# First operands loaded in halves and a shorter warm-up, in a hybrid-mixer layer

## The chip, the cores and the metric

The kernel runs on one core of a Trainium2 chip. The core has a matrix engine (TensorE, PE in the profile, with its weight loads as PEld), three engines for elementwise work (VectorE, DVE; ScalarE, ACT; GpSimd, POOL), a queue engine (SyncE, SP) that mostly starts transfers, and 16 DMA engines. The metric is the device time of one execution in microseconds.

## The reference

One layer, input x of 512 tokens by 1024 channels in float32. What matters here is its front:

```python
h = rmsnorm(x, norm_g[l])                      # x * rsqrt(mean(x*x) + eps) * g
p = jnp.einsum('btd,dc->btc', h, w_in[l])      # one input projection for all branches
(gq, gk, gv, gz, ggate, dq, dk, dv, dgate, qi, ki, wi, pu, pgate) = split_cols(p)
...                                            # gated linear attention, top-k attention, pooling
y = jnp.concatenate([y_gla, y_dsa, y_pool], axis=-1)
x = x + jnp.einsum('btc,cd->btd', y, w_out[l])
```

The output is a final rmsnorm of x. Every product is wanted at about float32 accuracy, so the kernel splits each operand into a high and a low part and multiplies three times: high by high, high weights by low tokens, low weights by high tokens.

## The kernel before

The projection is worked in column chunks. The first chunk of 512 columns (`FIRST`: the linear attention's q and k, the index k and some small pieces) is done in `open_run`, while the input is still arriving; the other chunks follow in `project`. In `open_run` the 1024 channels are 8 blocks, k = 0 to 7, of 128 channels. A block is a piece of x transposed, `xk` (128 channels by 512 tokens; `x0` for k = 0, with the eight columns of norm_g behind it), and a piece of the weights, `wk` (128 channels by 512 columns), 256 KB each. `load_x` and `load_w` start the transfers, wk0 and wk1 from ScalarE's queue, the others from SP's.

For each block `split` makes four operands: the high weights `whk` (ScalarE, `hi_of`, L96), the high tokens `hTh` (VectorE for k = 0, L958; ScalarE after that, L956), the low tokens `hTl` (VectorE, L959) and the low weights `wlk` (VectorE, `lo_of`, L99). In the text a number behind a name is the block: wlk2 is `wlk` of block 2. `square` lets ScalarE square x (L965) and GpSimd add the squares to `acc` (L967). `products` issues twelve matmuls per block, three parts by four groups of 128 tokens, into four accumulators `pns` (`pf` in the profile), each 128 tokens by 512 columns, filled over all eight blocks. Ahead of the first product come four products of ones in plain float32 (`warm`, L994), which nothing reads. After block 7, `rms` sums `acc` over the channels (`ss`, L980) and takes the power −0.5 on GpSimd (`rstd`, L983); `store_first` scales the four accumulators out to `ki` and `kq` (L272, L274), which are then transposed (L306, L299), and the index products `is` (L436) use the result.

The order on each engine is fixed when the program is built: TensorE's stream of block products is interleaved there with products of the next chunk, `qd` (`pt_qd`, L208 to L210), by a timeline that the builder works out. SP issues its transfers in the order of the code. Transfers on the hardware queues share eight semaphores in turn, DMAHW0 to DMAHW7, so a transfer waits for the one issued eight places before it.

Of the kernel before, what the change touches and what calls it, by code (L numbers as in the profile page):

```python
# [69 lines left out]
def hybrid_layer(  # L70
# [16 lines left out]
    def S(tag, shape, dt=F32, bufs=1, name=None):  # L87
        return sb.tile(shape, dt, tag=tag, name=name or tag, bufs=bufs)
# [6 lines left out]
    def hi_of(dst, src, scale=1.0):  # L95
        nc.scalar.activation(dst, src, AF.Copy, scale=scale)  # L96
# [832 lines left out]
    def open_run():  # L929

        xs, ws, wh, wl = {}, {}, {}, {}
        acc = S("acc", [P, T])
        pns = [PS("ov", [P, T], 1, name="pf0"), PS("sc", [P, T], 2, name="pf1"), PS("sc", [P, T], 2, name="pf2"),
               PS("pj", [P, T], 3, name="pf3")]
        ht = lambda parts, k: parts[k // 4][:, k % 4, :]
        x0 = S("x0", [P, T + KT])
        g_of = lambda k: x0[:, T + k:T + k + 1]

        def load_x(k):
            if k == 0:  # L940
                xs[0] = x0[:, 0:T]
                nc.sync.dma_start(x0, block(x_t, 0, T + KT))
                return
            xs[k] = S("xk", [P, T], bufs=5, name=f"xk{k}")
            nc.sync.dma_start(xs[k], block(x_t, k * P * T + P * KT, T))

        def load_w(k, eng=nc.sync):
            ws[k] = S("wk", [P, T], bufs=5, name=f"wk{k}")
            eng.dma_start(ws[k], block(w_in, k * P * T, T))

        def split(k):
            wh[k] = S("whk", [P, T], F32R, bufs=3, name=f"whk{k}")
            wl[k] = S("wlk", [P, T], F32R, bufs=3, name=f"wlk{k}")
            hi_of(wh[k], ws[k])
            if k:
                nc.scalar.activation(ht(hTh, k), xs[k], AF.Copy, scale=g_of(k))  # L956
            else:
                nc.vector.tensor_scalar(ht(hTh, k), xs[k], g_of(k), None, op0=ALU.mult)  # L958
            nc.vector.scalar_tensor_tensor(ht(hTl, k), xs[k], g_of(k), ht(hTh, k).bitcast(F32),  # L959
                                           op0=ALU.mult, op1=ALU.subtract)  # L960
            lo_of(wl[k], ws[k], wh[k])

        def square(k):
            q = acc if k == 0 else S("sqk", [P, T], bufs=2, name=f"sqk{k}")
            nc.scalar.activation(q, xs[k], AF.Square)  # L965
            if k:
                nc.gpsimd.tensor_tensor(acc, acc, q, op=ALU.add)  # L967

        def products(k, parts=range(3)):
            for part in parts:  # L970
                a, w = ht(hTl if part == 1 else hTh, k), (wl if part == 2 else wh)[k]
                for t in range(NT):
                    mm(pns[t], a[:, t * P:(t + 1) * P], w, start=(k + part == 0),  # L973
                                    stop=(k == KT - 1 and part == 2))

        def rms():

            ss = PS("tp", [P, NT], 2, name="ss")
            for t in range(NT):
                mm(ss[:, t:t + 1], acc[:, t * P:(t + 1) * P], ones[:, 0:1], start=True, stop=True,  # L980
                   skip_group_check=True)
            nc.vector.tensor_scalar(rstd, ss, 1.0 / D, EPS, op0=ALU.mult, op1=ALU.add)
            nc.gpsimd.tensor_tensor(rstd, rstd, half_neg, op=ALU.pow)  # L983

        load_x(0)
        load_w(0, nc.scalar)
        for k in range(1, KT):
            load_w(k, nc.scalar if k == 1 else nc.sync)
            load_x(k)
        nc.sync.dma_start(tab, table)  # L990
        load_next()
        load_next()
        for n in (4, 4, 2, 1):
            mm(warm[:, 0:n * P], ones, ones4[:, 0:n, :], start=True, stop=True)  # L994
        split(0)
        square(0)
        for k in range(KT - 1):
            products(k)
            if k + 1 < KT:
                split(k + 1)  # L1000
                square(k + 1)
            if k == 4:
                split_half(chunks[0], 0)
            if k == 6:
                split_half(chunks[0], 1)
                products(7, (0,))
                rms()
                half("n1", 0)
                products(7, (1, 2))
        for t in range(NT):  # L1010
            store_first(t, pns[t])
        rms_diag()
        store_rest()
# [59 lines left out]
def _x_blocks(x_t, norm_g):  # L1073

    import numpy as np

    first = np.concatenate([x_t[0:P], norm_g.reshape(KT, P).T], axis=1)
    return np.concatenate([first.reshape(-1), x_t[P:].reshape(-1)])


def _blocks(w, cols):
# [6 lines left out]
def _layout(i):  # L1088
# [4 lines left out]
    return {  # L1093
        "in_x": i["x"],
        "in_x_t": _x_blocks(i["x"][0].T, i["norm_g"][0]),
        "in_w_in": np.concatenate([w_in[:, FIRST].reshape(-1)] + [_blocks(w_in, cols) for _, cols in CHUNKS]),
        "in_w_out": np.concatenate([_blocks(w_out, list(range(256 * j, 256 * j + 256))) for j in range(4)]),
        "in_rel_bias": _bias_layout(i["rel_bias"]),
        "in_table": _small_layout(i["gla_gate_w2"], i["gla_gate_b"], i["gla_norm_g"], i["pool_w"], i["pool_scale"]),
# [26 lines left out]
```

## Time and profile before

| | |
|---|---|
| three runs | 262.27 us median, 262.04 to 262.34 |
| profiled execution | 262.02 us, span 260.2 us |
| TensorE busy | 245.0 us (94% of the span) |
| VectorE, ScalarE, GpSimd busy | 197.4, 119.6, 103.3 us |
| chain that ended last | TensorE 47%, VectorE 36%, waits without a cause shown 6%, ScalarE 4%, DMA 3% |

A busy time says how long an engine was at work, not whether the end waited for it. That is in the chain that ended last, which is followed back from the last instruction through whatever released each step. Matmul ends are modelled and overlap, so the distance from one start to the next tells the pace.

### The profile page before, as it was taken

The page shows a single profiled execution, that of the slowest core. Times are in us where ns is not written, and L with a number is a line of the kernel's source. Part 1 is how long each engine was busy: PE and PEld are TensorE (multiplying, and loading weights), DVE is VectorE, ACT ScalarE, POOL GpSimd, SP SyncE. Part 2 cuts the span into 40 slices and gives each one's busy share as a digit, 9 for nine tenths or more (in the row PEclk, how much of TensorE's full clock was granted, in tenths as well). Part 3 has the DMA queues.
Part 4 walks back from the last instruction along what each step waited for, and adds up shares of the span by engine and source line. Part 5 has one row for each costly group of instructions (what it writes and reads, how often), then busy time and mean ns, then how long its engine had stood idle before and what let it go on. Part 6 is the DMA issues. An engine that isn't in the chain of part 4 may idle for free.

```text
span 260.2 us, 4199 instructions
## 1 busy us (share of the span) xinstructions
PE 245.0 (94%) x1498; PEld 203.8 (78%) x1498; DVE 197.4 (76%) x442; ACT 119.6 (46%) x251; POOL 103.3 (40%) x109
## 2 busy tenths in 40 slices
PE   8999999999999999899999989998989978999990
PEld 4778889999999998688888867776756755788890
DVE  3999388899999999998999853599875877345322
ACT  5965186884836722225323353434465745222111
POOL 1645356354058630418534063618456562000011
PEclk9999999999999999999999999999999999999997
DMA  6994413225202150222314867605486000025012
GB/s 229 393 410 174 128 46 97 79 78 214 81 1 89 74 165 0 81 82 81 90 74 115 195 136 174 273 0 131 141 217 239 4 0 0 3 98 215 35 58 81
DMA packets 11780, 31.09 MB, mean 119 GB/s; under 512 B 1600, under 2 KB 1600, under 8 KB 11760
## 3 DMA queue, kind: packets, MB, share of 16 engines
q1 hardware_dynamic: 11328, 30.05, 36.2%
q10 hardware_dynamic: 432, 0.79, 0.9%
q8 instruction: 12, 0.20, 0.3%
q14 instruction: 8, 0.07, 0.1%
HBM read 23.91 MB, written 2.10 MB: 100 GB/s over the span
## 4 chain that ended last, share of the span: by engine, by line
PE 47%; DVE 36%; issue 6%; ACT 4%; DMA 3%; POOL 2%; SPq 1%; POOLq 0%; ACTq 0%; DVEq 0%
PE op L772 11%; DVE scs L459 8%; DVE m L458 6%; PE pf L973 5%; DVE ol L99 3%; PE pt_c L210 2%; PE pt_c L208 2%; PE pt_c L209 2%; DVE pm L583 2%; PE ov L741 2%; DMA wk<-in_w_in 2%; PE tpp L730 2%; ACT L L712 2%; DVE wl_n L99 2%; DVE wlk L99 2%
## 5 line engine op out<-in xcount | busy, mean ns | idle before, releaser
L721 POOL TENSOR_SCALAR L<-L,ast 128x128 f32<-128x128 f32 (+3 forms) x24 | 14.8, 630 | 34.1 <-DVE ast L719 34.1
L458 DVE MAX8 m<-scs 128x8 f32<-128x256 f32 (+2 forms) x48 | 26.5, 552 | 0.1
L459 DVE MATCH_REPLACE8 scs<-m,scs 128x256 f32<-128x256 f32 (+2 forms) x48 | 26.1, 543 | 0.0
L196 PE MATMUL pn_n<-wh_n,hTh 128*128 128x270 f32 (+1 forms) x128 | 21.6, 291 | 0.0
L196 PE MATMUL pn_n<-wl_n,hTh 128*128 128x270 f32 (+1 forms) x128 | 21.1, 287 | 0.0
L196 PE MATMUL pn_n<-wh_n,hTl 128*128 128x270 f32 (+1 forms) x128 | 21.0, 286 | 0.0
L712 ACT ACTIVATE L<-L,ast 128x128 f32<-128x128 f32 (+3 forms) x24 | 13.3, 557 | 16.0 <-DVE ast L710 15.1
L208 PE MATMUL pt_c<-hTh,wh_c 128*128 128x512 f32 x48 | 19.3, 402 | 0.0
L210 PE MATMUL pt_c<-hTh,wl_c 128*128 128x512 f32 x48 | 19.0, 395 | 0.0
L209 PE MATMUL pt_c<-hTl,wh_c 128*128 128x512 f32 x48 | 18.9, 394 | 0.0
L196 PEld LDWEIGHTS pn_n<-wh_n,hTh 128*128 128x128 f32 x128 | 18.2, 189 | 0.7 <-issue 0.4
L196 PEld LDWEIGHTS pn_n<-wl_n,hTh 128*128 128x128 f32 x128 | 18.0, 189 | 0.0
L196 PEld LDWEIGHTS pn_n<-wh_n,hTl 128*128 128x128 f32 x128 | 18.0, 189 | 0.0
L99 POOL TENSOR_TENSOR wl_c<-wr_c,wh_c 128x1024 fp32r<-128x1024 f32 x5 | 11.9, 2399 | 12.5 <-ACT wh_c L96 8.2
L967 POOL TENSOR_TENSOR acc<-acc,sqk 128x512 f32<-128x512 f32 x7 | 10.3, 1475 | 11.2 <-ACT sqk L965 11.2
L96 ACT ACTIVATE yDh<-yt 128x128 fp32r<-128x128 f32 x12 | 3.7, 310 | 21.8 <-DVE yt L744 21.8
L744 DVE TENSOR_TENSOR yt<-ov,dg 128x128 f32<-128x128 f32 x12 | 3.4, 285 | 13.2 <-PE ov L741 13.2
L99 POOL TENSOR_TENSOR wl_n<-wr_n,wh_n 128x1080 fp32r<-128x1080 f32 (+1 forms) x4 | 10.1, 2536 | 7.1 <-ACT wh_n L96 5.1
L689 POOL TENSOR_TENSOR L<-scs,TB 128x512 f32<-128x512 f32 x9 | 12.9, 1436 | 0.0
L778 ACT ACTIVATE sqo<-xr 128x512 f32<-128x512 f32 (+1 forms) x8 | 4.8, 604 | 16.9 <-DVE xr L777 10.6
L558 POOL TENSOR_TENSOR gss<-gss,hneg 128x4 f32<-128x4 f32 x4 | 4.1, 1014 | 21.4 <-DVE gss L557 21.4
L99 DVE TENSOR_TENSOR ol<-wr_wo,oh 128x512 fp32r<-128x512 f32 x16 | 11.2, 744 | 1.3 <-ACT oh L96 1.3
(241 smaller groups left out, 711.1 us busy)
## 6 DMA issues: line engine op xcount, KB each, us to landing
wr_wo<-in_w_out SPq DMA_DIRECT2D x8, 512.0 KB, 4.5
wr_c<-in_w_in SPq DMA_DIRECT2D x6, 512.0 KB, 3.9
wr_n<-in_w_in SPq DMA_DIRECT2D x4, 540.0 KB, 7.8
wr_n<-in_w_in SPq DMA_DIRECT2D x4, 536.0 KB, 3.5
xr<-in_x SPq DMA_DIRECT2D x4, 512.0 KB, 6.3
xk<-in_x_t SPq DMA_DIRECT2D x7, 256.0 KB, 5.5
wk<-in_w_in SPq DMA_DIRECT2D x6, 256.0 KB, 5.4
KK<-qkh SPq DMA_DIRECT2D x12, 128.0 KB, 2.5
```

The costliest lines, as they stand in the source:

```text
L99: return (eng or nc.vector).tensor_tensor(dst, src, hi.bitcast(F32), op=ALU.subtract)
L196: mm(ps[:, 0:n], a[:, k, ts_], w[:, k, :], start=(h + part + k == 0), stop=(h == 1 and part == 2 and k == 3))
L208: mm(ps[:, t0:T], c.hi[h][:, k, cs], hTh[h][:, k, t0:T], start=(h + k == 0), stop=False)
L209: mm(ps[:, t0:T], c.hi[h][:, k, cs], hTl[h][:, k, t0:T], start=False, stop=False)
L210: mm(ps[:, t0:T], c.lo[h][:, k, cs], hTh[h][:, k, t0:T], start=False, stop=(h == 1 and k == 3))
L458: nc.vector.max(out=m8, in_=msk[i])
L459: nc.vector.match_replace(out=msk[i], in_to_replace=m8, in_values=msk[i], imm_value=TAKEN)
L689: nc.gpsimd.tensor_tensor(L[:, :, near], msk[i][:, near].unsqueeze(1).to_broadcast([P, 2, 256]), TB[:, 2 * g:2 * g + 2, :], op=ALU.subtract)
L712: nc.scalar.activation(L[:, b, 0:n], L[:, b, 0:n], AF.Exp, bias=st[:, b:b + 1], scale=-1.0, accum_out=st[:, 2 + b:3 + b])
L721: nc.gpsimd.tensor_scalar(L[:, b, 0:n], L[:, b, 0:n], st[:, 4 + b:5 + b], 1.0, op0=ALU.mult, op1=ALU.mult)
L772: mm(outs[t][a][:, 0:e - a], lhs, rhs, start=(first and yi == 0 and rhs is wh and lhs is yh), stop=(last and yi == len(ys) - 1 and lhs is yl))
L973: mm(pns[t], a[:, t * P:(t + 1) * P], w, start=(k + part == 0), stop=(k == KT - 1 and part == 2))
```

## The change

Block 0 of x and of the weights comes in two transfers each, and the host lays the bytes out so that each half is contiguous (the gains g now stand in front of the first half of x0). Block 0's high weights and high tokens are made in two halves of 256 columns. The four products of high by high of block 0 become eight of 256 columns, the first tokens and the first weight columns first. Of the four warm-up products, the two of 256 and 128 columns are dropped.

```diff
-        x0 = S("x0", [P, T + KT])
-        g_of = lambda k: x0[:, T + k:T + k + 1]
+        x0 = S("x0", [P, KT + T])
+        g_of = lambda k: x0[:, k:k + 1]
+        H = T // 2
 
         def load_x(k):
             if k == 0:
-                xs[0] = x0[:, 0:T]
-                nc.sync.dma_start(x0, block(x_t, 0, T + KT))
+                xs[0] = x0[:, KT:KT + T]
+                nc.sync.dma_start(x0[:, 0:KT + H], block(x_t, 0, KT + H))
+                nc.sync.dma_start(x0[:, KT + H:KT + T], block(x_t, P * (KT + H), H))
                 return
...
         def load_w(k, eng=nc.sync):
             ws[k] = S("wk", [P, T], bufs=5, name=f"wk{k}")
+            if k == 0:
+                for a in (0, H):
+                    eng.dma_start(ws[0][:, a:a + H], block(w_in, a * P, H))
+                return
             eng.dma_start(ws[k], block(w_in, k * P * T, T))
 
         def split(k):
...
-            hi_of(wh[k], ws[k])
             if k:
+                hi_of(wh[k], ws[k])
                 nc.scalar.activation(ht(hTh, k), xs[k], AF.Copy, scale=g_of(k))
             else:
-                nc.vector.tensor_scalar(ht(hTh, k), xs[k], g_of(k), None, op0=ALU.mult)
+                for a in (0, H):
+                    hi_of(wh[0][:, a:a + H], ws[0][:, a:a + H])
+                    nc.vector.tensor_scalar(ht(hTh, 0)[:, a:a + H], xs[0][:, a:a + H], g_of(0), None, op0=ALU.mult)
...
         def products(k, parts=range(3)):
             for part in parts:
                 a, w = ht(hTl if part == 1 else hTh, k), (wl if part == 2 else wh)[k]
+                if k + part == 0:
+                    for t, c in ((0, 0), (1, 0), (0, H), (1, H), (2, 0), (3, 0), (2, H), (3, H)):
+                        mm(pns[t][:, c:c + H], a[:, t * P:(t + 1) * P], w[:, c:c + H], start=(c == 0), stop=False,
+                           skip_group_check=True)
+                    continue
                 for t in range(NT):
-                    mm(pns[t], a[:, t * P:(t + 1) * P], w, start=(k + part == 0),
-                                    stop=(k == KT - 1 and part == 2))
+                    mm(pns[t], a[:, t * P:(t + 1) * P], w, start=False, stop=(k == KT - 1 and part == 2),
+                       skip_group_check=True)
...
-        for n in (4, 4, 2, 1):
+        for n in (4, 4):
             mm(warm[:, 0:n * P], ones, ones4[:, 0:n, :], start=True, stop=True)
```

TensorE's stream at its start, before (`warm` is the warm-up, `pf0` to `pf3` the accumulators, `whk0` and `hTh0` the high parts of block 0):

```order
L994 MATMUL warm_68<-ones_63 128x512 x2
L994 MATMUL warm_68<-ones_63 128x256
L994 MATMUL warm_68<-ones_63 128x128
L973 MATMUL pf0_143<-whk0_192,hTh0_77 128x512
L973 MATMUL pf1_144<-whk0_192,hTh0_77 128x512
L973 MATMUL pf2_145<-whk0_192,hTh0_77 128x512
L973 MATMUL pf3_146<-whk0_192,hTh0_77 128x512
```

And with the change:

```order
L1007 MATMUL warm_68<-ones_63 128x512 x2
L982 MATMUL pf0_143<-whk0_192,hTh0_77 128x256
L982 MATMUL pf1_144<-whk0_192,hTh0_77 128x256
L982 MATMUL pf0_143<-whk0_192,hTh0_77 128x256
L982 MATMUL pf1_144<-whk0_192,hTh0_77 128x256
L982 MATMUL pf2_145<-whk0_192,hTh0_77 128x256
```

Two warm-up products are gone, and the first four products need the first half of the tokens only, the first two of them the first half of the weight columns only.

SP's queue at its start, before, with what each transfer waits for (`x` is block 0 of x):

```order
L942 DMA x_147<-in_x_t 128x520
L945 DMA xk_153<-in_x_t 128x512
L949 DMA wk_155<-in_w_in 128x512
L945 DMA xk_157<-in_x_t 128x512
L949 DMA wk_159<-in_w_in 128x512
L945 DMA xk_161<-in_x_t 128x512
L949 DMA wk_163<-in_w_in 128x512 [waits DMAHW0_49]
```

And with the change:

```order
L943 DMA x_147<-in_x_t 128x264
L944 DMA x_147<-in_x_t 128x256
L947 DMA xk_155<-in_x_t 128x512
L955 DMA wk_157<-in_w_in 128x512
L947 DMA xk_159<-in_x_t 128x512
L955 DMA wk_161<-in_w_in 128x512 [waits DMAHW0_49]
L947 DMA xk_163<-in_x_t 128x512 [waits DMAHW1_49]
```

Two transfers of block 3 (wk_161 and xk_163 here) now wait, for the first half of wk0 and of x0; from wk4 on each waits for the same landing as before.

TensorE's stream around the sum of squares `ss`, before (`pt_qd` is the next chunk, `whk_320` block 6, `whk_341` block 7):

```order
L973 MATMUL pf_146<-whk_320,hTh_78 128x512
L210 MATMUL pt_qd_407<-hTh_77,wl_qd_305 128x384 [waits DVE_49]
L208 MATMUL pt_qd_407<-hTh_77,wh_qd_304 128x384
L209 MATMUL pt_qd_407<-hTl_79,wh_qd_304 128x384
L210 MATMUL pt_qd_407<-hTh_77,wl_qd_305 128x384
L208 MATMUL pt_qd_407<-hTh_77,wh_qd_304 128x384
L973 MATMUL pf_143<-whk_320,hTl_80 128x512 [waits DVE_49]
...
L973 MATMUL pf_146<-whk_341,hTh_78 128x512
L209 MATMUL pt_qd_407<-hTl_79,wh_qd_304 128x384
L980 MATMUL ss<-ones,acc 128x1 [waits Pool_49]
```

And with the change (from the fifth `pt_qd` product of the piece on, `whk_326` is block 6 and `whk_347` block 7):

```order
L208 MATMUL pt_qd_413<-hTh_77,wh_qd_310 128x384
L209 MATMUL pt_qd_413<-hTl_79,wh_qd_310 128x384
L210 MATMUL pt_qd_413<-hTh_77,wl_qd_311 128x384
L208 MATMUL pt_qd_413<-hTh_77,wh_qd_310 128x384
L209 MATMUL pt_qd_413<-hTl_79,wh_qd_310 128x384
L986 MATMUL pf_143<-whk_326,hTl_80 128x512 [waits DVE_49]
...
L986 MATMUL pf_146<-whk_347,hTh_78 128x512
L210 MATMUL pt_qd_413<-hTh_77,wl_qd_311 128x384
L208 MATMUL pt_qd_413<-hTh_78,wh_qd_356 128x384 [waits Activation_49]
L209 MATMUL pt_qd_413<-hTl_80,wh_qd_356 128x384
L993 MATMUL ss<-ones,acc 128x1 [waits Pool_49]
```

Of the `pt_qd` products, nine instead of five stand between block 6's first and second part, and three instead of one directly ahead of `ss`: six more in front of it, and six fewer behind. Elsewhere the order on every engine is the same.

## Rows read from the trace of the kernel before

**Rows 1.** Chain that ended last, 0 to 37 us: start, us, what.

```profile
1.21 4.53 DMA wk<-in_w_in
...
5.76 0.64 ACT whk L96
...
14.54 1.78 DVE wlk L99
...
16.37 6.80 PE pf L973 x28
```

**Rows 2.** Timeline, TensorE, 0 to 22 us: start, us, engine, line, operation [idle before].

```profile
5.20 1.17 PE L973 MATMUL pf<-whk,hTh 128*128 128x512 f32 x4
...
11.81 1.09 PE L973 MATMUL pf<-whk,hTl 128*128 128x512 f32 x4
12.98 1.20 PE L973 MATMUL pf<-wlk,hTh 128*128 128x512 f32 x4
...
14.92 1.07 PE L973 MATMUL pf<-whk,hTl 128*128 128x512 f32 x4
16.37 1.21 PE L973 MATMUL pf<-wlk,hTh 128*128 128x512 f32 x4 [0.38 <-DVE wlk L99]
```

**Rows 3.** Timeline, VectorE, 0 to 22 us.

```profile
4.25 0.49 DVE L958 TENSOR_SCALAR hTh<-x 128x512 fp32r<-128x512 f32 x1 [3.25 <-DMA x<-in_x_t]
...
7.04 0.75 DVE L959 SCALAR_TENSOR_TENSOR hTl<-xk,x,hTh 128x512 fp32r<-128x512 f32 x1 [0.92 <-ACT hTh L956]
7.71 1.80 DVE L99 TENSOR_TENSOR wlk<-wk,whk 128x512 fp32r<-128x512 f32 x1
...
11.14 1.79 DVE L99 TENSOR_TENSOR wlk<-wk,whk 128x512 fp32r<-128x512 f32 x1
```

**Rows 4.** Timeline, ScalarE, 0 to 22 us.

```profile
4.42 0.63 ACT L96 ACTIVATE whk<-wk 128x512 fp32r<-128x512 f32 x1 [1.77 <-DMA wk<-in_w_in]
4.96 0.62 ACT L965 ACTIVATE acc<-x 128x512 f32<-128x512 f32 x1
5.76 0.64 ACT L96 ACTIVATE whk<-wk 128x512 fp32r<-128x512 f32 x1 [0.19 <-DMA wk<-in_w_in]
```

**Rows 5.** Timeline, GpSimd, 0 to 22 us.

```profile
7.62 1.35 POOL L967 TENSOR_TENSOR acc<-acc,sqk 128x512 f32<-128x512 f32 x1 [6.32 <-ACT sqk L965]
```

**Rows 6.** Timeline, TensorE's weight loads, 0.9 to 5.6 us.

```profile
3.76 0.34 PEld L994 LDWEIGHTS warm<-ones 128*128 128x128 f32 x1 [0.52 <-issue]
4.61 0.64 PEld L994 LDWEIGHTS warm<-ones 128*128 128x128 f32 x3 [0.52 <-issue]
```

**Rows 7.** DMA, 8 to 13 us, then 17 to 20 us: packets moved.

```profile
DMA packets 1087, 1.98 MB, mean 397 GB/s; under 512 B 118, under 2 KB 118, under 8 KB 1087
...
DMA packets 329, 1.25 MB, mean 416 GB/s; under 512 B 40, under 2 KB 40, under 8 KB 329
```

**Rows 8.** Windows: length, busy by engine, granted clock, DMA share, GB/s.

```profile
1.50:2.75 1.25, 1.25 (x2) 0.37 (x2) 0.00 (x0) 1.14 (x2) 0.00 (x0) 1.00 0.74 169
2.75:5.25 2.50, 2.50 (x8) 1.26 (x6) 0.97 (x2) 0.83 (x2) 0.00 (x0) 1.00 1.02 375
```

**Rows 9.** Chain and timelines around the sum of squares: TensorE, GpSimd and VectorE.

```profile
31.07 0.18 PE pt_qd L210
...
28.16 0.95 PE L980 MATMUL ss<-ones,acc 128*128 128x1 f32 x8
...
29.38 2.02 POOL L983 TENSOR_TENSOR rstd<-rstd,hneg 128x4 f32<-128x4 f32 x1 [6.52 <-DVE rstd L982]
...
32.55 0.74 DVE L274 TENSOR_SCALAR kq<-pf,rstd 128x512 f32<-128x512 f32 x1
...
34.16 1.04 PE L299 MATMUL tpn<-ident,kq 128*128 128x128 f32 x8
...
38.85 0.40 PE L436 MATMUL is<-KS,QS 96*128 96x256 f32 x2
```

**Rows 10.** Window 35 to 60 us.

```profile
35.00:60.00 25.00, 25.00 (x164) 22.67 (x163) 22.30 (x43) 19.87 (x37) 11.29 (x15) 1.00 0.22 70
```

More of the change, by code (lines that the diff above doesn't have):

```diff
@@ L1075, in _x_blocks, with _first @@
     import numpy as np
-    first = np.concatenate([x_t[0:P], norm_g.reshape(KT, P).T], axis=1)
-    return np.concatenate([first.reshape(-1), x_t[P:].reshape(-1)])
+    first = np.concatenate([norm_g.reshape(KT, P).T, x_t[0:P, 0:T // 2]], axis=1)
+    return np.concatenate([first.reshape(-1), x_t[0:P, T // 2:].reshape(-1), x_t[P:].reshape(-1)])
+def _first(w):
+    import numpy as np
+    return np.concatenate([w[0:P, 0:T // 2].reshape(-1), w[0:P, T // 2:].reshape(-1), w[P:].reshape(-1)])
 def _blocks(w, cols):
@@ L1095, in _layout @@
         "in_x_t": _x_blocks(i["x"][0].T, i["norm_g"][0]),
-        "in_w_in": np.concatenate([w_in[:, FIRST].reshape(-1)] + [_blocks(w_in, cols) for _, cols in CHUNKS]),
+        "in_w_in": np.concatenate([_first(w_in[:, FIRST])] + [_blocks(w_in, cols) for _, cols in CHUNKS]),
         "in_w_out": np.concatenate([_blocks(w_out, list(range(256 * j, 256 * j + 256))) for j in range(4)]),
```

## The prediction

> **What bounds the kernel now.** I read the chain of waits first, since it says which work set the end, and only then the engines' timelines of the first 22 us. The chain does not begin with TensorE. It begins with the transfer of the second weight block, wk1, issued at 1.21 and on the chain for 4.53 us; ScalarE's split of that block follows at 5.76, then VectorE's chain of low parts down to the one that starts at 14.54, and only at 16.37 does the chain pass to TensorE, for 28 products in one unbroken run [rows 1]. So in the opening TensorE works, but the end does not wait for it.
>
> The timelines say why. ScalarE takes wk0 at 4.42, the first square at 4.96, and then stands idle for 0.19 us until wk1 has landed at 5.74 [rows 4]. VectorE is idle for 0.92 us before hTl1 at 7.04, waiting for ScalarE's hTh1 [rows 3]. From there VectorE falls behind: wlk1 takes 1.80 us and wlk2 1.79, where hTl1 took 0.75 [rows 3]. GpSimd's addition of squares starts at 7.62 and takes 1.35, to 8.97 [rows 5]; wlk1, which starts at 7.71, ends at 9.51, about half a microsecond after GpSimd is done. So VectorE gets about one operation through per addition, the additions follow ScalarE's squares, and the squares follow wk1. VectorE owes two operations per block. A product of 512 columns takes 6.80/28 = 0.243 us in the long run [rows 1], four of them 0.97. TensorE meets VectorE's delay at wlk2: the four hTl2 products start at 11.81, so 12.78 would do, and it starts at 12.98 (0.2 waited). It meets it again at wlk3: 14.92 + 0.97 = 15.89, started at 16.37 (0.48 waited) [rows 2].
>
> The Trainium skill says the same as a rule and against this change: in "SBUF — State Buffer", section "SBUF: two separate sides", VectorE operations with two SBUF inputs and GpSimd operations take a shared pair of ports as an exclusive lock, for the whole instruction. By that rule the additions hold the low parts up as a block, not in proportion, and a TensorE that starts earlier cannot loosen them. The rows agree (1.80 us beside GpSimd, 0.75 before it).
>
> **The change part by part.** The sum is made against the profiled execution, 262.02 us (span 260.2 and 1.8 around it); the median of the three runs is 262.27, so I add 0.25 at the end.
>
> *Two warm-up products less.* Four passes of 512 columns start 0.85 us apart and the last of them ends at 4.61; the 256- and 128-column products stand from 4.61 to 5.20 [rows 2, 6]. They go: TensorE is free 0.59 us earlier.
>
> *First halves.* Their 264 KB (0.27 MB) are the first bytes: 169 GB/s over 1.25 us bring 0.21 MB by 2.75, and the rest at 375 GB/s is there at 2.91 [rows 8]. By the same rule the whole 0.53 MB is moved at 3.60, and it was taken at 4.25 (x0) and 4.42 (wk0) [rows 3, 4], 0.65 to 0.8 later; so the halves are taken at about 3.6 to 3.7. Half of the 0.49 us multiplication and somewhat over half of the 0.63 us split end by about 4.1. That is before 4.61, so TensorE's first product starts at 4.61 instead of 5.20: a lead of 0.59 us.
>
> *Eight products of 256 columns for four of 512.* No such row of the product exists here. 384 columns take 0.18 us [rows 9] and 512 take 0.243, so 256 come to about 0.12, and eight to 0.96, as the four now; the upper end, no saving per product at all, would be 1.9. The second weight half lands with the bytes of the old wk0, at about 4.4, is split by about 4.8, and is wanted at 4.85. I take 0. Should it cost the whole 0.97, TensorE is 0.38 behind its present place at hTl0, and the waits at wlk2 and wlk3 (0.68 together) take that up.
>
> *Where the lead goes.* With it TensorE reaches wlk2 at 12.78 − 0.59 = 12.19. VectorE's wlk2 ends at 11.14 + 1.79 = 12.93 [rows 3] as long as wk1 lands when it did. TensorE then waits 0.8 instead of 0.2 and goes on at 12.98, exactly as now. The gain of the first two parts is 0 at the end: VectorE's chain, started by wk1, is what is late next.
>
> *wk1 itself.* It is now third on ScalarE's queue instead of second, issued about 0.45 later (one issue), with the same bytes ahead of it, since wk0 is still moving then. ScalarE reaches it after two half splits and the square, at about 5.35. So each microsecond of wk1's landing counts in full, in both directions: down to −0.42 (from 5.76 to 5.35), and up by what 256 extra packets cost. In steady flow 2 KB rows take 16 × 5 / 969 = 83 ns per packet and engine (1087 packets less 118 small ones) and rows of about 4.3 KB 16 × 3 / 289 = 166 ns [rows 7]; the straight line through both leaves 7 ns per packet, so 256 more on 16 engines add 0.11 us. If a packet's time did not depend on its size, they would add 16 × 83 ns = 1.3 us. The row nearest to 1 KB is the 2 KB one, and the line through both rows is nearly all bytes: I take +0.1.
>
> *SP's queue.* wk3 and xk3 now wait for the first halves to land, because eight transfers may be open and two more are in front; they leave at about 3.7 and 4.0 instead of 2.57 and 3.05. Queued behind them are wk4 and later blocks, which wait for the same landings as now. What hides it: at 3.7 about 1 MB issued earlier is still to move, 2.8 us at 375 GB/s. I take 0; without that cover, up to 0.3.
>
> *TensorE's order near the sum of squares.* Six products of the qd projection now stand ahead of ss. At 0.18 each that is 1.05 us: ss moves from 28.16 to 29.2 [rows 9]. VectorE's reciprocal input, GpSimd's power (2.02 us from 29.38) and the stores behind them move by the same 1.05: the last kq store, now over at 32.55 + 0.74 = 33.29, ends at 34.34 [rows 9]. The six products are the ones that no longer stand behind, so TensorE arrives at the kq transposes where it does now, 34.16 to 34.3, and waits about 0.1. The index products at 38.85 [rows 9] then have about 0.3 left. Bounds: 0, and 1.05 were the cover gone. I take +0.1. From 35 to 60 TensorE is busy for all 25.00 us [rows 10], so a small shift of another engine there is absorbed.
>
> Sum: 0 + 0 + 0.1 + 0 + 0.1 = +0.2: 262.2 by the profiled execution, 262.4 to 262.5 by the median. I give 262.4.
>
> **The rivals.**
>
> *The lead is kept (faster).* For it: TensorE is nearly always busy in the first 16 us, and 0.59 us of its work is gone. Against it: the two waits on wlk in rows 2. It needs wk1 to land earlier, which moves ScalarE, GpSimd and VectorE together. It would give −0.42 to −0.59: 261.7 to 261.85.
>
> *wk1 lands late (slower).* One mechanism, on ScalarE's DMA queue: the rows of half the size are limited by their number rather than their bytes. For it: in the first 1.25 us the rate is 169 GB/s, less than half of the 375 after it [rows 8], so something other than bytes limits there; if it is the packet count, 0.1 MB is missing at 2.75, worth 0.28 us, and with 1.3 us at the far end I put it at +0.65: 262.9. It decides from a landing of wk1 0.5 us later than 5.74. Against it: the straight line of rows 7.
>
> *The clock.* The granted clock reads 1.00 in both stretches of rows 8, yet a 512-column warm-up pass takes 0.85 us (1.67 ns a column) up to 4.61, and the 768 columns after it 0.59 us (0.77 ns) [rows 2, 6]: the pace of the lower level, 1.2 GHz, and then that of 2.4. Up to 4.61 TensorE gets the same instructions in both kernels, so I expect the upper level at 4.61 again. If all of the first block's work (twelve products of 512 columns) ran at the lower one, it would take 2 × 12 × 0.243 = 5.8 us and end at 10.4 instead of 5.20 + 2.9 = 8.1, and after the waits at wlk2 and wlk3 (0.68) leave +1.6: 263.9. The Trainium skill states in "TensorE: Matmul & The Clock Gate", section "Part 1: The HAM clock gate (the \"warmup\" mystery)", that the array starts throttled and activity frees it, which speaks against a shorter warm-up; what it would make of the time is this rival. The rows on the pace agree with it, the granted clock does not show it.
>
> **How the numbers follow.** About 0.2% (0.52 us) is what a measurement of this kernel can tell from no change. The lead eaten up: 0.58, with its own range 261.9 to 262.8. The lead kept: 0.17. wk1 late: 0.20. The clock: 0.05. The later reshuffle of waits can carry the likeliest case over either bound, 0.04 each. So faster 0.17 + 0.04 = 0.21, slower 0.20 + 0.05 + 0.04 = 0.29, same 0.50. The range 261.6 to 263.1 takes in the kept lead and the middle of the late wk1, and leaves out the clock and the far end of wk1.
>
> **What would show it.** Right: the first product near 4.6; wlk2's products near 13.0 with a wait of about 0.8 us for VectorE ahead of them; wlk3's near 16.4; ScalarE's second weight split near 5.8, still waiting for wk1; ss about one microsecond later and no gap at the transposes beyond 0.2. Wrong: the second weight split well before 5.7 (then faster) or after 6.2 (then slower), the run of 28 products not starting near 16.4, or a first product at twice its present duration.

## The result, and the profile after

The changed kernel takes 264.24 us (median of 6 runs, 262.86 to 264.77), the kernel before on the same chip 262.15 (6 runs, 261.93 to 262.50): a ratio of 1.0073, with a 95% interval of 1.0048 to 1.0098. The forecast was 262.4, no change, with a range of 261.6 to 263.1. The profiled run took 264.58 us, with a span of 262.7 against 260.2.

The chain of waits of the changed kernel (start, length, what) still begins with wk1's transfer; it answers to [rows 1]:

```profile
1.64 6.34 DMA wk<-in_w_in
...
8.00 0.63 ACT whk L96
...
16.74 1.79 DVE wlk L99
...
18.57 6.77 PE pf L986 x28
```

The transfer stands on the chain for 6.34 us instead of 4.53, and was issued 0.43 later (1.64 for 1.21). ScalarE's split of wk1 starts at 8.00 instead of 5.76, the run of 28 products at 18.57 instead of 16.37. These are 2.24 and 2.20 us, and the span is 2.5 longer: so nearly all of the loss is there before VectorE's chain has begun.

ScalarE's timeline, changed kernel, as [rows 4]:

```profile
3.80 0.42 ACT L96 ACTIVATE whk<-wk 128x256 fp32r<-128x256 f32 x1 [1.15 <-DMA wk<-in_w_in]
4.40 0.42 ACT L96 ACTIVATE whk<-wk 128x256 fp32r<-128x256 f32 x1 [0.18 <-DMA wk<-in_w_in]
4.72 0.62 ACT L973 ACTIVATE acc<-x 128x512 f32<-128x512 f32 x1
8.00 0.63 ACT L96 ACTIVATE whk<-wk 128x512 fp32r<-128x512 f32 x1 [2.65 <-DMA wk<-in_w_in]
```

The halves did what they were to do: the first is taken at 3.80, before the 4.42 of the whole block. Then ScalarE stands for 2.65 us where it stood for 0.19. TensorE's timeline shows who pays, as [rows 2]:

```profile
4.27 1.59 PE L982 MATMUL pf<-whk,hTh 128*128 128x256 f32 x8
5.70 1.09 PE L986 MATMUL pf<-whk,hTl 128*128 128x512 f32 x4
...
9.29 1.20 PE L986 MATMUL pf<-whk,hTh 128*128 128x512 f32 x4 [1.56 <-ACT hTh L962]
...
11.78 1.20 PE L986 MATMUL pf<-wlk,hTh 128*128 128x512 f32 x4 [0.36 <-DVE wlk L99]
...
18.57 1.21 PE L986 MATMUL pf<-wlk,hTh 128*128 128x512 f32 x4 [0.32 <-DVE wlk L99]
```

The first product starts at 4.27, 0.93 us earlier than before. TensorE uses this up waiting 1.56 us for block 1, and still meets VectorE's low parts at each following block.

What the DMA engines did meanwhile, in windows of the kernel before and then of the changed one (length, busy by engine, granted clock, DMA share, GB/s):

```profile
2.75:3.75 1.00, 1.00 (x2) 0.34 (x1) 0.00 (x0) 0.00 (x0) 0.00 (x0) 1.00 1.04 379
3.75:6.25 2.50, 2.50 (x11) 1.75 (x10) 1.85 (x3) 1.64 (x3) 0.00 (x0) 1.00 0.93 332
```

```profile
2.75:3.75 1.00, 1.00 (x2) 0.34 (x1) 0.16 (x1) 0.00 (x0) 0.00 (x0) 1.00 1.04 350
3.75:6.25 2.50, 2.50 (x13) 1.84 (x12) 1.90 (x4) 1.36 (x3) 0.00 (x0) 1.00 0.76 222
```

While the halves flow, in the first window, the rate is 350 GB/s against 379, so rows of 1 KB are not what takes 2 us. Once they are done, and nearly all rows are of 2 KB again, the engines are busy for 0.76 of the time and move 222 GB/s, though four transfers of 256 KB had been issued by 3.00. After that, in a DMA view of 6.25 to 7.5 us (queue 1 is SP's, queue 10 ScalarE's: packets, MB, share of the 16 engines), the end of wk1 gets little:

```profile
q1 hardware_dynamic: 223, 0.41, 91.3%
q10 hardware_dynamic: 22, 0.03, 7.5%
```

### The profile page after: what moved, and what is told of

The parts are those of the page before. It is cut to its first block, busy times and chain, and to the rows that moved or that the text cites. A ratio compares the mean times of both kernels' runs of the same rounds, so it can differ in the third digit from the quotient of the medians.

```text
span 262.7 us, 4195 instructions
## 1 busy us (share of the span) xinstructions
PE 245.1 (93%) x1498; PEld 203.2 (77%) x1498; DVE 196.9 (75%) x443; ACT 119.5 (45%) x252; POOL 103.6 (39%) x109
## 4 chain that ended last, share of the span: by engine, by line
PE 44%; DVE 37%; issue 6%; DMA 3%; ACT 3%; POOL 2%; SPq 1%; POOLq 0%; ACTq 0%; DVEq 0%
PE op L772 11%; DVE scs L459 8%; DVE m L458 6%; PE pf L986 4%; DVE ol L99 3%; DMA wk<-in_w_in 2%; PE pt_c L210 2%; DVE pm L583 2%; PE pt_c L208 2%; PE pt_c L209 2%; PE ov L741 2%; PE tpp L730 2%; DVE L L710 2%; DVE wl_n L99 2%; PE pt_pu L208 1%
## 5 line engine op out<-in xcount | busy, mean ns | idle before, releaser
L975 POOL TENSOR_TENSOR acc<-acc,sqk 128x512 f32<-128x512 f32 x7 | 10.9, 1559 | 12.8 <-ACT sqk L973 12.8
```

## The experiments

First all runs in one table. "Ahead" counts the transfers that were issued, on either queue, before wk1; the split is ScalarE's start on wk1 in the profiled run, with its wait for the transfer just before (0 where the profile shows none). Each ratio is to runs of the kernel before on the same chip.

| kernel | ahead of wk1 | split of wk1 (wait) | median us | ratio to before, 95% interval |
|---|---|---|---|---|
| before | 3 | 5.76 (0.19) | 262.1 to 262.2 | |
| changed | 5 | 8.00 (2.65) | 264.24 | 1.0048 to 1.0098 |
| e1_whole_loads | 3 | 5.73 (0) | 261.94 | 0.9985 to 1.0003 |
| e2_halves_only | 5 | 7.01 (1.41) | 263.26 | 1.0027 to 1.0060 |
| e3_x_halves | 3 | 5.21 (0) | 260.89 | 0.9941 to 0.9989 |
| e4_w_halves | 5 | 7.83 (1.75) | 263.78 | 1.0047 to 1.0092 |
| e5_x_only | 3 | 5.03 (0) | 262.03 | 0.9984 to 1.0009 |
| e6_dummy_act | 5 | 7.72 (2.27) | 263.89 | 1.0047 to 1.0082 |
| e7_hold_sp | 3 | 5.44 (0.23) | 262.35 | 0.9989 to 1.0026 |
| e8_wk1_second | 2 or 3 | 7.63 (0, behind wk0b) | 264.11 | 1.0066 to 1.0100 |
| e9_x_one | 3 | 5.79 (0.45) | 261.96 | 0.9984 to 1.0003 |
| e10_x_one_short | 3 | 5.46 (0.37) | 261.77 | 0.9982 to 1.0000 |
| e11_both_one | 3 | 5.74 (0) | 262.12 | 0.9988 to 1.0006 |
| e12_w_one | 3 | 5.53 (0.20) | 262.08 | 0.9987 to 1.0006 |
| e13_tiny_act | 5 | 7.05 (1.29) | 263.13 | 1.0029 to 1.0058 |
| e14_hold_act | 6 | 8.76 (3.17) | 264.93 | 1.0094 to 1.0120 |
| e15_tiny_sp | 3 | 5.49 (0) | 261.80 | 0.9976 to 0.9995 |
| e16_x_halves_again | 3 | 5.36 (0) | 260.81 | 0.9939 to 0.9982 |
| e17_pp_tp | 3 | 5.67 (0) | 260.98 | 0.9944 to 0.9971 |
| e18_best | 3 | 5.92 (0.23) | 260.99 | 0.9946 to 0.9971 |

### Is it the loads at all?

**e1_whole_loads.** The changed kernel with x0 and wk0 in whole transfers again; short warm-up, half splits and 256-column products stay.

```diff
-                nc.sync.dma_start(x0[:, 0:KT + H], block(x_t, 0, KT + H))
-                nc.sync.dma_start(x0[:, KT + H:KT + T], block(x_t, P * (KT + H), H))
+                nc.sync.dma_start(x0, block(x_t, 0, KT + T))
-            if k == 0:
-                for a in (0, H):
-                    eng.dma_start(ws[0][:, a:a + H], block(w_in, a * P, H))
-                return
```

> The changed kernel with x0 and wk0 in one transfer each, as before; the half splits, the eight products of 256 columns and the short warm-up stay. Theory A (the halved transfers make wk1 land late, and that is the loss): wk1's split on ScalarE starts at 5.8 again and the time is within 0.5 us of the kernel before, 261.8 to 262.7. Theory B (the loss comes from the shorter warm-up, the smaller products or the moved sum of squares): about 264, with wk1's split at 5.8.

Measured 261.94, no change. TensorE in this kernel:

```profile
4.88 1.29 PE L977 MATMUL pf<-whk,hTh 128*128 128x256 f32 x8
...
12.94 1.19 PE L981 MATMUL pf<-wlk,hTh 128*128 128x512 f32 x4 [0.24 <-DVE wlk L99]
...
16.35 1.21 PE L981 MATMUL pf<-wlk,hTh 128*128 128x512 f32 x4 [0.36 <-DVE wlk L99]
```

The first product is 0.32 earlier than before and wlk3 is where it was (16.37): with wk1 on time the lead is eaten by VectorE's chain, as forecast, and the warm-up, the half splits and the eight products cost nothing. Without the halved loads there is no loss. One part is tested by half only: in e1 the builder put three more `qd` products in front of `ss`, not six (`ss` at 28.64, 0.48 later than before).

**e2_halves_only.** The opposite: the kernel before with only the halved loads (the diff is that of the change without its lines on splits, products and warm-up).

> The kernel before with x0 and wk0 in two transfers each and nothing else changed (whole splits, products of 512 columns, four warm-up products). Theory A: wk1's split starts near 8.0 instead of 5.76 and the time is 263.5 to 264.7. Theory B: wk1's split near 5.8 and 262.0 to 262.5.

263.26, and the split at 7.01, short of the 8.0 expected: the loads alone cost 1.1 us, about half of the change's 2.1. Why the same loads delay the split by 1.25 us here and by 2.24 in the changed kernel isn't shown; the runs of each spread over about 2 us.

**e3_x_halves** and **e4_w_halves.** The changed kernel with only x0, or only wk0, in halves; the other block's loads as in e1.

> The changed kernel with only x0 in halves; wk0 comes in one transfer, so wk1 is second on ScalarE's queue again. Theory A1 (wk1 is late because it is third on ScalarE's queue): within 0.5 us of the kernel before, split at 5.8. Theory A2 (each extra early transfer costs about the same, whichever queue it is on): about 263.2, split near 6.9. Theory A3 (the small rows of x0 are the cause): 264, split near 8.0.

> The changed kernel with only wk0 in halves; x0 comes in one transfer. Theory A1: 264, wk1's split near 8.0. Theory A2: about 263.2, split near 6.9. Theory A3: within 0.5 us of the kernel before, split near 5.9.

They went opposite ways: wk0 alone in halves is nearly as slow as the change (263.78), and x alone in halves is faster than both kernels (260.89), which none of the three theories had. In the DMA view of 2.5 to 4 us, x in halves first, then wk0 in halves:

```profile
q10 hardware_dynamic: 202, 0.38, 66.2%
q1 hardware_dynamic: 225, 0.20, 38.9%
```

```profile
q1 hardware_dynamic: 199, 0.38, 68.0%
q10 hardware_dynamic: 170, 0.16, 31.7%
```

I read this as a share by row size: both queues move about as many packets, so the one with the longer rows moves twice the bytes. The Trainium skill, "DMA: Bandwidth & Descriptors", section "Queues, rings and completion order", has the engines alternate between queues packet by packet, which seemed to agree, though a packet there holds several descriptors and so need not be one of the profile's. The theory fell later (e9, e12).

**e5_x_only.** The kernel before with x0 in halves and nothing else.

> The kernel before with one edit: the first block of x comes in two halves on SP's queue; the weights' first block stays whole, the warm-up full, the first split and products whole. Share theory (the two queues take turns row by row, so the queue with the longer rows moves more bytes): ScalarE's 2 KB rows beside SP's 1 KB rows carry about twice the bytes from 2.5 to 4 us, wk1 has landed by about 5.0 and its split starts at 5.2 to 5.3; wlk3 ends about 0.3 to 0.5 us earlier than before's 16.37 and the time is 260.7 to 261.7. Rival, that the gain of x in halves alone came from the shorter warm-up and the split in halves: wk1 may land early, but TensorE, whose first product cannot start before its warm-up ends at about 5.2, makes nothing of it, and the time is 262.0 to 262.4.

The split came at 5.03, even a little earlier than expected, and the time did not follow (262.03): it is the one that the rival gave. ScalarE:

```profile
5.03 0.62 ACT L96 ACTIVATE whk<-wk 128x512 fp32r<-128x512 f32 x1
7.58 0.72 ACT L958 ACTIVATE hTh<-xk,x 128x512 fp32r<-128x512 f32 x1 [1.93 <-DMA xk<-in_x_t]
```

Now xk1 is late, the third transfer on SP's queue and the fifth of all. That run took 263.12, the slowest of ten; the fastest took 261.12.

### Rows, bytes, or the place in the order?

**e6_dummy_act.** The kernel before, nothing halved, with one unused transfer of 64 KB ahead of wk1:

```diff
         load_w(0, nc.scalar)
+        dz = S("dz", [P, P])
+        nc.scalar.dma_start(dz, block(x_t, 0, P))
```

> The kernel before with nothing halved, and one unused transfer of 128 rows of 512 bytes (64 KB) put on ScalarE's queue between wk0 and wk1, so that wk1 is the third on that queue and the sixth or so of all, with its own rows of 2 KB. Theory of place (what counts is that wk1 is no longer among the first four transfers): the split of wk1 waits for its transfer and starts at 7.0 or later, and the time is about 263 to 264.5. Theory of halves (half-sized rows are what slows the opening): wk1 lands later only by the 64 KB ahead of it, about 0.2 to 0.4 us, its split starts at 5.9 to 6.2 and the time is 262.2 to 262.7.

263.89 and a split at 7.72: without any halved row, the extra transfer costs 1.7 us. At the 375 GB/s of [rows 8] its 64 KB are 0.17 us of traffic. With them wk1's issue moved from 1.21 to 1.64, just behind that of wk2 (1.62), so 256 KB more went ahead too; e4 has the same order.

**e7_hold_sp.** e4 with SP's second issue held by a one-element write of ScalarE into xk1:

```diff
             xs[k] = S("xk", [P, T], bufs=5, name=f"xk{k}")
+            if k == 1:
+                nc.scalar.activation(xs[1][:, 0:1], lead, AF.Copy)
```

> The changed kernel with x0 whole and wk0 in halves, and SP's second block (xk1) held back until ScalarE has begun its work, so that wk0a, x0, wk0b and wk1 are the first four transfers and wk1 is still the third on ScalarE's queue. Theory of the first four of all: wk1 lands at about 5 us and its split starts at 5.2 to 5.8, against 7.83 without the hold. Theory of the third on a queue: wk1 still lands at 7 to 8 and its split starts there. In both xk1 comes late (it is issued some 1.5 us later), so the time itself tells less than the split: 262 to 264.

wk1 is third on its queue as in e4, but fourth of all, and is split at 5.44 instead of 7.83. So it is not the third place on a queue. That SP's queue was empty meanwhile would also explain it.

**e8_wk1_second.** The changed kernel with ScalarE's queue in the order wk0a, wk1, wk0b.

> The changed kernel with both blocks in halves, but ScalarE's queue ordered wk0a, wk1, wk0b: wk1 is second on its queue, the second half of wk0 third. Theories of place (first four of all, or third on a queue): wk1 lands at 4.5 to 5.2, and wk0b is the late one, at 6 or later, so ScalarE's split of the second half waits about 2 us and holds everything behind it: 264 or more. Theory that halving slows whatever follows: wk1 lands late too, at 6.5 or later.

```profile
3.74 0.42 ACT L96 ACTIVATE whk<-wk 128x256 fp32r<-128x256 f32 x1 [0.60 <-DMA wk<-in_w_in]
6.78 0.42 ACT L96 ACTIVATE whk<-wk 128x256 fp32r<-128x256 f32 x1 [2.63 <-DMA wk<-in_w_in]
7.11 0.62 ACT L974 ACTIVATE acc<-x 128x512 f32<-128x512 f32 x1
7.63 0.62 ACT L96 ACTIVATE whk<-wk 128x512 fp32r<-128x512 f32 x1
```

The lateness has moved to wk0b, half as large and now with five transfers ahead of it. What stands there is late, at half the size too.

**e9_x_one, e10_x_one_short, e11_both_one, e12_w_one.** Rows of half the size without an extra transfer: one DMA reads two rows per partition. For x0 (e9: in the kernel before; e10: in the changed one with wk0 whole), for wk0 (e12: in the kernel before), for both (e11: the changed kernel, all else kept):

```diff
+                nc.sync.dma_start(x0.rearrange("p (h c) -> p h c", h=2), rows(x_t, 0, (KT + T) // 2))
...
+                eng.dma_start(ws[0].rearrange("p (h c) -> p h c", h=2), rows(w_in, 0, H))
```

> The kernel before with one edit: the first block of x is still one transfer, but each of its 2080-byte rows is sent as two of 1040 bytes; no extra transfer, no split, product or warm-up changed. Theory of place and share together: ScalarE's queue gets about twice SP's bytes from 2.5 to 4 us, so the split of wk0 starts at 3.8 to 4.0 and that of wk1 by 5.2; x0, wk0, wk1 and xk1 are the first four transfers, so xk1 too is there when ScalarE wants it (by 5.9, no wait, against 1.93 us of wait in the kernel that halved x in two transfers), wlk3 ends its wait at 15.9 to 16.1 and the time is 260.4 to 261.4. Rival (the share comes from the extra transfer, not from the row size): opening as before, 262.0 to 262.3.

> The changed kernel with wk0 whole in 2048-byte rows and x0 one transfer of two 1040-byte rows per partition; the short warm-up, the split in halves and the 256-column products are kept. If the spread of the version with x in two transfers (seven runs near 260.5, three near 262.5) came from xk1, its fifth transfer, landing late in some runs, all runs are now near each other, at 260.2 to 261.0. If the spread has another cause, some runs still lie at 262.3 to 262.8.

> The changed kernel, all of it, but the halves of x0 travel as one transfer and those of wk0 too: the same bytes in the same 1 KB rows, two transfers fewer. Theory of place: wk1 is again among the first four transfers, its split starts at 5.9 or before, and the time is 261.7 to 262.3. Theory that 1 KB rows on both queues are what costs: split of wk1 at 7 or later and 263.5 to 264.5.

> The kernel before with one edit, the mirror of the one-transfer split of x: wk0 is still one transfer, but each 2048-byte row is sent as two of 1024; x0 whole. Theory of share: ScalarE's queue now moves about half of SP's bytes from 2.5 to 4 us, wk0 lands some 0.4 us later, the split of wk1 starts at 6.0 to 6.6 after a wait and the time is 262.4 to 263.2. Rival (row size does not set the share): opening as before, 262.0 to 262.3.

e11 is the key. ScalarE in it, and the window that answers to those above:

```profile
4.39 0.72 ACT L96 ACTIVATE whk<-wk 128x256 fp32r<-128x256 f32 x2 [1.66 <-DMA wk<-in_w_in]
5.01 0.61 ACT L974 ACTIVATE acc<-x 128x512 f32<-128x512 f32 x1
5.74 0.63 ACT L96 ACTIVATE whk<-wk 128x512 fp32r<-128x512 f32 x1
```

```profile
2.75:3.75 1.00, 1.00 (x2) 0.34 (x1) 0.00 (x0) 0.00 (x0) 0.00 (x0) 1.00 1.01 346
3.75:6.25 2.50, 2.46 (x8) 1.40 (x7) 1.97 (x4) 1.75 (x4) 0.00 (x0) 1.00 1.06 389
```

The same bytes in the same 1 KB rows, in two transfers fewer: 262.12, split at 5.74, 346 GB/s while the 1 KB rows flow (350 in the changed kernel), and 389 GB/s behind them where the changed kernel moved 222. The 2 us belong to the two transfers more, not to the rows.

e9 and e12 missed: 261.96 and 262.08 where a share by row size gave 260.4 to 261.4 and 262.4 to 263.2. In e12, with the longer rows on SP's queue, the queues of 2.5 to 4 us read

```profile
q1 hardware_dynamic: 162, 0.30, 55.2%
q10 hardware_dynamic: 272, 0.26, 49.9%
```

so ScalarE's queue moved 272 packets to SP's 162 and nearly the same bytes. So row size by itself does not set the share. e10 (261.77) missed both its ranges: its runs lie within 0.51 us, as expected without a late xk1, but not at 260.2 to 261.0, and its opening is only 0.3 us shorter.

**e13_tiny_act** and **e15_tiny_sp.** The kernel before with an unused transfer of only 16 rows of 512 bytes (8 KB), on ScalarE's queue ahead of wk1, or on SP's ahead of xk1:

```diff
         load_w(0, nc.scalar)
+        dz = S("dz", [16, P])
+        nc.scalar.dma_start(dz, bass.AP(tensor=x_t.tensor, offset=x_t.offset, ap=[[P, 16], [1, P]]))
```

> The kernel before, nothing halved, and one unused transfer of 16 rows of 512 bytes (8 KB) on ScalarE's queue between wk0 and wk1. Count theory (the first four transfers flow at full rate, the fifth and later start with a lull, whatever their size): wk1 is the fifth, lands late, its split starts at 6.8 or later and the time is 263 to 264.4. Byte theory (it was the 64 KB ahead of wk1, or the half-sized blocks, that took the time): 8 KB are 0.02 us at 370 GB/s, the split starts at 5.7 to 5.9 and the time is 262.0 to 262.4.

> The kernel before, nothing halved, and the unused 8 KB transfer on SP's queue between x0 and xk1. Count theory: the first four are now x0, wk0, the small one and wk1, so wk1 lands sooner than before (4.5 to 5.0, split at 5.5 without a wait), xk1 is the late one, and ScalarE's pass over xk1 waits 0.5 to 2 us for it in at least some runs: 261.5 to 263.5 with a spread of over 0.8 us. Byte theory: no change, 262.0 to 262.4, spread under 0.6 us.

With 8 KB put ahead of wk1 the kernel takes 1.05 us longer (263.13 against 262.08). SP's issue of wk2, ScalarE's issue of wk1 and the split in e13:

```profile
1.62 0.43 SPq L949 DMA_DIRECT2D wk<-in_w_in  x1
...
1.63 0.44 ACTq L949 DMA_DIRECT2D wk<-in_w_in  x1
...
7.05 0.63 ACT L96 ACTIVATE whk<-wk 128x512 fp32r<-128x512 f32 x1 [1.29 <-DMA wk<-in_w_in]
```

The count is met, but e13 doesn't rule bytes out: wk1's issue came 0.42 us later than before, 0.01 behind that of wk2, so 264 KB overtook it, 0.72 us at 375 GB/s. The changed kernel and e2 do rule them out: there the same bytes as before stand ahead of wk1, in two transfers more. Nor is the later issue the whole reason: from issue to split it is 3.8 to 4.7 us in every profile with at most three transfers ahead (e8 left out), e7 with its issue at 1.64 among them, and 5.3 to 6.4 with five or six.

The same 8 KB on SP's queue put xk1 and not wk1 behind: the split is at 5.49 without a wait, and the time 0.28 us better. What counts is who is overtaken. The expected late xk1 did not show in the profiled run (its pass started at 6.01, straight behind the split), and the spread of 1.48 us is the only sign of it.

**e14_hold_act.** The kernel before with wk1's issue held by a one-element write, as in e7, to 2.92 us; it is second on ScalarE's queue.

> The kernel before, with ScalarE's issue of wk1 held until it has run its first activations (issue at 2.7 instead of 1.2), so that wk1 is still the second transfer on its queue but comes behind xk1, wk2 and xk2 in the order of issue. If the count is one of all queues together (four), wk1 falls behind it: split at 7 or later, 263 or more. If it is two on each queue, wk1 starts about 1.9 us after its issue, as others did, at 4.5, takes half of some 370 GB/s and lands at about 5.9: split at 6.0 to 6.4, 262.3 to 262.8.

```profile
2.92 0.37 ACTq L951 DMA_DIRECT2D wk<-in_w_in  x1
4.44 0.63 ACT L96 ACTIVATE whk<-wk 128x512 fp32r<-128x512 f32 x1 [1.55 <-DMA wk<-in_w_in]
4.98 0.61 ACT L967 ACTIVATE acc<-x 128x512 f32<-128x512 f32 x1
8.76 0.63 ACT L96 ACTIVATE whk<-wk 128x512 fp32r<-128x512 f32 x1 [3.17 <-DMA wk<-in_w_in]
```

The latest of all, 5.8 us after its issue, with only wk0 before it on its own queue: the place counts over both queues together. That fits the Trainium skill, "DMA: Bandwidth & Descriptors", section "Issuing engines are not separate DMA queues", by which transfers run on the same 16 engines whichever engine issued them.

### Why x alone in halves is faster

**e16_x_halves_again.** e3 once more, on another chip.

> The version with x0 in two transfers and wk0 whole, once more on this chip, the fastest so far (260.89). If it holds up: a median of 260.3 to 261.3, with most runs near 260.5 and some near 262.5, those in which xk1, its fifth transfer, lands late. If the earlier result was one chip's luck: 262 or more.

260.81: it holds up, in two groups again (eight runs at 259.95 to 261.11, four at 262.46 to 263.94). But the profiled run took 262.67 with xk1 on time (at 5.88), so a late xk1 isn't what put it in the slower group. From 219.40 to 222.81 us, e3 (260.91) and then e16:

```profile
219.40:222.81 3.41, 3.41 (x24) 2.58 (x24) 1.25 (x4) 0.68 (x2) 0.60 (x1) 1.00 0.00 0
```

```profile
219.40:222.81 3.41, 3.41 (x18) 2.42 (x17) 0.29 (x1) 0.75 (x2) 0.75 (x2) 0.50 0.00 0
```

In e16 TensorE's granted clock reads 0.50 in this stretch, the lower of its two levels (1.2 and 2.4 GHz), and 18 products start in it instead of 24. In the 3.4 us before it, TensorE was busy for 1.90 us in both profiles, at the upper level. The output products behind it (`op` with `yDh`) start at 222.63 instead of 221.00; 0.15 of this stood before the fall, and the rest is most of the 1.8 us between the two profiles. Of the six other runs near 262.5, four have a mean granted clock of 0.980 to 0.987, below the 0.992 to 0.998 of the fifteen runs near 260.5; for the two others (0.992 and 0.994) it is open.

Nor does the opening explain the gain. e3's wlk3 starts at 15.95 and e1's at 16.35, 0.40 apart, but the spans are 1.2 apart. The rest is near 195 us, at the two pooling products: e3 reaches them 0.21 us before e1 (193.08 and 193.29), and the transposes behind them (`tpp`, L730) 1.06 before it (198.01 and 199.07). The kernel before, and then e3:

```profile
193.36 1.13 PE L595 MATMUL pp<-pm,tab 128*128 128x512 f32 x2 [0.43 <-DVE yt L744]
195.41 1.13 PE L595 MATMUL pp<-pm,tab 128*128 128x512 f32 x2 [0.93 <-DVE ast L710]
```

```profile
193.08 1.99 PE L595 MATMUL pp<-pm,tab 128*128 128x512 f32 x4 [0.43 <-DVE yt L744]
```

A wait of 0.93 us for VectorE is missing in e3, though the order of TensorE's instructions there is the same. It is missing in e16 and e8 too, and present in the changed kernel. What in the compiled program decides this was not traced further.

**e17_pp_tp** and **e18_best.** That wait taken away by itself in the kernel before; and the same in e10:

```diff
-            ps = PS("sc", [P, T], 2, name=f"pp{j}")
+            ps = PS("tp", [P, T], 2, name=f"pp{j}")
```

> The kernel before with one edit some 190 us behind the opening, which stays as it was: the two accumulators of the pooling products (pp0, pp1) come from the pool of the transposes' banks instead of that of the score products. If the part of the x-halves version's gain that its opening does not explain (0.85 of its 1.2 us) is the wait of 0.93 us between these two products, which is missing there, then it goes here too: the two products follow each other, and the time is 261.1 to 261.5. If that gain has another source: 262.0 or more.

> Both findings together: x0 in one transfer of 1040-byte rows, wk0 whole, short warm-up and split halves (261.77 by itself), and the pooling accumulators from the transposes' banks. If the two add up: 260.7 to 261.1. If the scheduler's other waits take the second gain back: 261.5 or more.

e17 takes 260.98 (five runs, 260.82 to 261.03), a ratio of 0.9958 and a little less than expected: the pool of two accumulators, 190 us behind the opening, brings 1.1 us. In e17 the products read

```profile
192.93 2.05 PE L595 MATMUL pp<-pm,tab 128*128 128x512 f32 x4
```

and wait for nothing: both waits, 0.43 and 0.93, are gone. So about 0.8 of e3's 1.2 us is a side effect of how its program came out, and 0.4 at most its loads. e18 (260.99) lies in the range given for a sum of both, but is no better than e17: its split came at 5.92 in the profiled run, so its opening had no lead to add.

## Why the prediction was wrong

**Failed: "wk1 itself".** The term was +0.1 us (−0.42 to +1.3), worked from the number of packets; the split came 2.24 us later. The forecast saw the place that decides ("each microsecond of wk1's landing counts in full", deciding from 0.5 us late) and that wk1 had become third on its queue, but priced the 256 extra packets alone, and the place and the 0.45 us of later issue at nothing, because wk0 would still be moving. The price per packet held: from 2.75 to 3.75 us the changed kernel moved 326 packets of 1 KB or more in 1.04 of 16 engines' time, 51 ns each, where the straight line through [rows 7] gives 45 for 1 KB and 83 for 2 KB. What it left out is the two extra transfers that pass ahead of wk1: same bytes and rows in two transfers fewer, no loss (e11); one unused transfer ahead, 1.05 us (e13) and 1.7 us (e6), with wk2 let through as well. In every trace wk1 was split by 5.92 when at most three transfers had been issued before it and nothing of block 0 held it up, and at 7.01 or later with five or six before it. The upper bound of 1.3 us, too, was a bound on packets, and so not one on what happened.

**The rival "wk1 lands late"** was the right outcome with the wrong mechanism ("the rows of half the size are limited by their number") and too small a price: +0.65 forecast, about 2.1 measured.

**Right.** The halves (260 KB together, not 264) were taken at 3.59 (VectorE) and 3.80, forecast 3.6 to 3.7. The first product was forecast at 4.61 and came at 4.27, but the eight took 1.43 us up to the next group, not 0.96; that group starts at 5.70 where it started at 6.21, a lead of 0.51 for the 0.59 forecast. Before:

```profile
6.21 1.09 PE L973 MATMUL pf<-whk,hTl 128*128 128x512 f32 x4
```

The lead goes at wlk2 as long as wk1 is on time: e1 shows it by itself. SP's queue: wk3 leaves at 3.79, forecast 3.7, and e1, in which it leaves at 2.57, shows the rest without loss.

**The clock** cost nothing that shows. In the changed kernel and in e1 the groups of four products behind the first are 0.93 us apart from the start (5.70 and 6.63; 6.00, 6.93 and 7.87), the pace of the upper level. But the level comes late in some runs, whatever the warm-up: the trace's record of the granted clock starts, at the upper level, between 4.02 and 7.18 us in the ten profiles with the long warm-up and between 3.96 and 6.95 in the ten with the short one (4.88 in the changed kernel). Ahead of it there is no record, and the views print 1.00. In e11 it starts at 6.58, and the eight products take 1.82 us up to the next group:

```profile
4.86 1.98 PE L983 MATMUL pf<-whk,hTh 128*128 128x256 f32 x8
```

With 262.12 that was absorbed; the rival's 1.6 us were not seen. In two experiments the clock fell again in the opening: e14, after TensorE had waited 1.87 us for block 1, reads 0.50 from 11.29 to 14.70, and e8, after a wait of 2.19, from 8.10 to 11.51. In e14 `ss` is 2.96 us later than before, no more than the split of wk1 (3.00); for e8 the cost is not separated.

**The order near ss** was forecast to move ss by 1.05 us and cost 0.1. TensorE in the changed kernel:

```profile
31.35 0.95 PE L993 MATMUL ss<-ones,acc 128*128 128x1 f32 x8
...
37.78 1.12 PE L927 MATMUL rb<-diag,ones 128*128 128x512 f32 x2 [0.46 <-DVE qil L99]
```

ss moved by 31.35 − 28.16 [rows 9] = 3.19, of which 2.20 are the opening: 0.99. A wait of 0.46 stands at rb, larger than forecast and inside the bounds of 0 to 1.05. In sum: 2.2 at the opening and up to 0.46 here cover the 2.5 us of the span. No other profile has a wait at rb, neither with three products moved and a late opening (e4) nor with none moved and a later one (e14), so it goes with the six.

**Open.** Why a transfer with five ahead of it is so slow: the rows show engines partly idle (0.76 busy), and then SP's queue with 91.3% of them, but not what holds wk1's packets back. By the packet records of the traces, wk1's first row moves at 3.60 us in the changed kernel and at 3.76 before; the last is done at 7.46 and at 5.27. So the transfer does not start late, it is slow. With four ahead (xk1 in e3, e5, e15, e16) it was late in one profile of four. Whether e7's early wk1 owes more to its place or to the idle SP queue was not separated.

## What to carry to other kernels

Before cutting a transfer in two, count the transfers that are then issued ahead of the next one the chain waits for: here that transfer (wk1, in e8 the second half of wk0) was waited for 1.3 to 3.2 us whenever five or six were ahead on both queues together, with no more bytes ahead than before in the changed kernel and e2. If the smaller piece isn't needed as a separate arrival, keep one transfer. And read a small gain to its place in the trace before crediting the edit: 0.8 of 1.2 us came from a wait 190 us away that the edit removed by accident, and that one line removes on purpose.

## What the runs showed of the hardware

- One unused 8 KB transfer ahead of wk1 went with 1.05 us of the kernel's time (e13); it also moved wk1's issue from 1.21 to 1.63 us, behind that of wk2.
- The same bytes ahead of wk1 in five transfers instead of three: its last row lands 2.2 us later, though its first moves as early (changed kernel against before).
- Stretches of mostly 1 KB rows ran at 346 GB/s (e11), 350 (changed kernel) and 382 (e2), against 379 for 2 KB rows (before), all from 2.75 to 3.75 us.
- The two queues' shares did not follow row size alone: 272 packets to 162 for nearly equal bytes (e12), and 202 to 225 for 0.38 to 0.20 MB (e3).
- A granted clock of 1.00 printed for the first microseconds stands for no record: the records start between 3.96 and 7.18 us, and the warm-up passes ahead of that run at 0.85 us per 512 columns [rows 6], the pace of the lower level.
- The clock can fall to its lower level in one execution and not in another of the same program; in e16 against e3 that took about 1.5 us.
